# Attention scores of two query tiles at once, from the two halves of TensorE's rows

## The chip, the cores and the metric

The kernel runs on one core of a Trainium2 chip. The metric is the device time of one execution in microseconds (us). The core has five engines with instruction streams of their own: TensorE (PE in the profile, its weight loads PEld), VectorE (DVE), ScalarE (ACT), GpSimd (POOL) and SyncE (SP), which issues nearly all DMAs. TensorE multiplies 128 rows at a time: the stationary operand (the weights) is loaded, the moving operand streams past, and the result lands in PSUM, of which a bank holds 512 float32 per partition.

## The reference

One layer of a bidirectional encoder on a grid of 16 x 64 tokens (1024 tokens, width 1024), in float32. An embedding LayerNorm is followed by one combined input projection; its columns are the query, key, value and gate of a neighbourhood attention, the input and gate of a bidirectional gated recurrence, and two merge gates. What the change touches is the attention:

```
q_rows = (q * scale).reshape(B, rows, GRID_W, H, Dh).transpose(1, 0, 2, 3, 4)
...
s = jnp.einsum('bqhd,bqnhd->bhqn', q_row, k_g).astype(jnp.float32) + bias[None]
p = jax.nn.softmax(s, axis=-1).astype(v.dtype)
return jnp.einsum('bhqn,bqnhd->bqhd', p, v_g)
```

There are 8 heads of 64 channels. Each token attends to a window of 8 x 16 tokens of the grid. Afterwards both branches are gated, projected, merged and projected again, and a last LayerNorm ends the layer.

## The kernel before, in words

**Precision.** Matrix products use the type float32r, which carries fewer bits than float32. Operands are therefore split in a high part and a low part (`lo_of`, line 119, makes the low part), and a product is made of three: high x high, low x high, high x low (`mm3`, line 122).

**Stages.** Up to about 110 us the kernel normalises x, turns it with TensorE and projects v and q. `q_hi`, `q_lo` and `q_store` (lines 327 to 338) write each 128-row block of q, its high and low parts side by side, to a DRAM tensor `q_d`, for one half of the tokens (512) at a time. From there to 430 us the 16 pairs of the remaining column blocks are projected by a table of seven products per pair, one per slot of about 2.7 us; among them `take_k` (line 651) splits k and writes it to `k_d` (line 666). The recurrence's work is threaded between these slots. From 430 to 541 us comes the attention, then the branch projections and the output projection with the last LayerNorm.

**Tiles of the attention.** The 1024 tokens are eight tiles of 128 (a strip of 8 grid columns). A query tile's keys lie in its own strip and its neighbours (`near`, line 51): three key tiles, or two at the ends. For head h, `load_q` puts the high part of q (64 rows) and the low part (64 rows) on top of each other, so that a tile `qs` has all 128 rows in use; `load_k` reads k twice, so that `ks` has the high part of k in both row halves, and behind it the low part in both. `score` (line 1026) then needs two products of 128 rows: stacked q against high k, and stacked q against low k. The sum has all four of high x high, low x high, high x low and low x low.

**Order of the attention.** One loop (line 1145) runs over units, eight per head, with one head of lead-in and three units (`PV_LAG`) at the end. TensorE executes in the order written; the other engines as well. In the unit (h, c) stand, in this order:

- VectorE reads the score of the unit before out of PSUM, adds the bias and takes the row minimum of the negative (`biased`, line 1033); it belongs to head h + 1
- VectorE makes the low part of the transposed probabilities of the unit before (`turned_lo`)
- TensorE transposes probabilities of head h (`turned`) and multiplies those of three units ago with v (`values`, line 1067)
- ScalarE makes the high part (`turned_hi`), then the exponential (`exped`, line 1044)
- TensorE makes one `score` of head h + 1; which query tile is in the table `SCORES`
- at the first unit of a head, SyncE issues the loads for head h + 2
- TensorE makes "fill" products, which belong to the other branch's projection (tile `mb`): 2 or 2.5 per unit, by the table `FILL`

In the lead-in (head 0's scores) only scores and fill products stand on TensorE. Scores have two PSUM buffers (tag "s"), and a product into one waits until VectorE has read it. The score tiles `sc` in SBUF have two buffers too. Once per head `sums_turned` (line 1094) turns the row sums with a product of 8 weight columns.

Of the kernel before, what the change touches and what calls it, by code (L numbers as in the profile page):

```python
# [9 lines left out]
F32 = mybir.dt.float32  # L10
F32R = mybir.dt.float32r
# [3 lines left out]
P = 128  # L15
S = 1024
D = 1024
NK = D // P
H = 8
DH = 64  # L20
GR, GC = 16, 64
NT = S // P
HALF = 512
# [13 lines left out]
HI_POOL = ("a12", "s2", "s1", "s3", "s4")  # L37
U_PAIRS = (0, 5)
BLOCKS = (1, 0, 6, 2, 3, 4, 5, 7)
SCORES = (0, 1, 2, 5, 6, 7, 3, 4)  # L40
PV_LAG = 3
FILL = (16, 20, 20, 20, 20, 20, 20, 20, 12)

# [3 lines left out]
HALVES = ((slice(0, 64), slice(64, P)), (slice(64, P), slice(0, 64)))  # L47
# [3 lines left out]
def near(t):  # L51

    return range(max(t - 1, 0), min(t + 2, NT))
# [13 lines left out]
def encoder_kernel(ctx, tc, x, gb1, gb, w_qk, w_v, w_s, w_ba, w_bb, w_gate, smalls, bias, w_out, out):  # L67
    nc = tc.nc
    V, A, G, PE, SP = nc.vector, nc.scalar, nc.gpsimd, nc.tensor, nc.sync
# [7 lines left out]
    dram = tc.alloc_tile_pool(name="dram", bufs=1, space=bass.MemoryType.DRAM)  # L77
# [6 lines left out]
    def bank(name):  # L84
        return banks[0].tile([P, HALF], F32, tag="bank", name=name)

    h_d = dram.tile([NT, P, D], F32, name="h_d")
    v_d = dram.tile([4, P, NT, 4 * DH], F32, name="v_d")
    q_d = dram.tile([H // 2, P, 2, S], F32, name="q_d")
    k_d = dram.tile([H // 2, P, 2, S], F32, name="k_d")  # L90
    rs_d = dram.tile([H, NT, P], F32, name="rs_d")
    za_d = dram.tile([4, P, S], F32, name="za_d")
    zb_d = dram.tile([4, P, S], F32, name="zb_d")
# [25 lines left out]
    def lo_of(eng, lo, full, hi):  # L119
        eng.tensor_tensor(lo, full, hi.bitcast(F32), ALU.subtract)  # L120
# [70 lines left out]
    halves = [slice(c * HALF, (c + 1) * HALF) for c in range(2)]  # L191
# [59 lines left out]
    def ti(i):  # L251
        return slice((i % 4) * P, (i % 4 + 1) * P)
# [82 lines left out]

    def q_store(m, n):
        qs = outs.pop(("q", m, n))
        SP.dma_start(q_d[m][:, :, halves[n]], qs[:].bitcast(F32))


    s_a, s_w = {}, {}
# [102 lines left out]
    pst = tc.alloc_tile_pool(name="pst0", bufs=4, space=bass.MemoryType.PSUM, reuse_waits="tile")  # L444
# [206 lines left out]
    def take_k(m0):  # L651

        def consume(mi, n, add, o, c=None):
            c = o if c is None else c
            if add is not None:
                V.tensor_tensor(c[:], add[:], o[:], ALU.add)
            tag, w = ("uc", S) if (mi, n) == (1, 1) else ("up", S + 3)
            t = lru.tile([P, w], F32R, tag=tag, bufs=2, name=f"k{m0}{mi}{n}")
            hi, lo = t[:, :HALF], t[:, HALF:S]

            def high():
                A.copy(hi, c[:])

            def store():
                lo_of(V, lo, c[:], hi)
                SP.dma_start(k_d[m0 + mi][:, :, halves[n]], t[:, :S].rearrange("p (z f) -> p z f", z=2).bitcast(F32))
            return [high, store]
        return consume

# [178 lines left out]

    def load_q(h):
        hd = late["hd" if h % 2 else "hd0"]  # L850
        q = hd.tile([P, S], F32R, tag="qs", name=f"qs{h}")
        bt = hd.tile([P, BIAS_W], F32, tag="bias", name=f"bias{h}")
        SP.dma_start(q[:].bitcast(F32), q_d[h // 2][HALVES[h % 2][0]].rearrange("p z s -> (p z) s"))
        SP.dma_start(bt[:], bias[h])
        heads[h] = q, bt

    def load_k(h):
        k = late["hd"].tile([P, 2, S], F32R, tag="ks", bufs=2, name=f"ks{h}")
        SP.dma_start(k[:].rearrange("p z s -> p (z s)").bitcast(F32),
                     k_d[h // 2][HALVES[h % 2][0]].rearrange("p z s -> p (z s)").unsqueeze(1).to_broadcast([DH, 2, 2 * S]))  # L860
        heads[h] = heads[h][0], k, heads[h][1]

    def load_head(h):
# [109 lines left out]
    for slot in range(7 * N_PAIR + 4):  # L973
        p, k = divmod(slot, 7)
# [30 lines left out]
    pst = tc.alloc_tile_pool(name="pst", bufs=1, space=bass.MemoryType.PSUM, reuse_waits="tile")  # L1005
# [13 lines left out]
    vvs, sums, scs, tps, pts, attns, rsb, gates = {}, {}, {}, {}, {}, {}, {}, {}  # L1019
# [3 lines left out]
            vvs[hp] = at0.tile([P, NT, 2, 2 * DH], F32R, tag="vv", bufs=2, name=f"vv{hp}")  # L1023
            SP.dma_start(vvs[hp][:].rearrange("p b e c -> p b (e c)").bitcast(F32), v_d[hp])

    def score(h, t):
        q, k, _ = heads[h]
        keys = slice(near(t).start * P, near(t).stop * P)
        o = scs[h, t] = pst.tile([P, HALF], F32, tag="s", bufs=2, name=f"s{h}_{t}")
        for z in range(2):  # L1030
            PE.matmul(o[:, :P * len(near(t))], q[:, t * P:(t + 1) * P], k[:, z, keys], start=z == 0, stop=z == 1)  # L1031

    def biased(h, t):

# [9 lines left out]
    def exped(h, t):  # L1044
        w = P * len(near(t))
        A.activation(probs[h % 2][t][:], scs.pop((h, t))[:, :w], AF.Exp, bias=sums[h][0][:, t:t + 1], scale=-1.0,  # L1046
                     accum_out=sums[h][1][:, t:t + 1])
# [97 lines left out]
    for unit in range(-NT, H * NT + PV_LAG):  # L1145
        h, c = divmod(unit, NT)
        before, b = divmod(unit - 1, NT)
        pv, pb = divmod(unit - PV_LAG, NT)

        if -1 <= before < H - 1:  # L1150
            biased(before + 1, SCORES[b])
        if 0 <= before < H:
# [16 lines left out]
        if -1 <= before < H - 1:  # L1169
            exped(before + 1, SCORES[b])  # L1170
        for f in pending:
# [2 lines left out]
        for f in todo.pop(unit, ()):  # L1174
            f()
        if -1 <= h < H - 1:
            score(h + 1, SCORES[c])
        if 0 <= h < H:
            if c == (4 if h == H - 1 else 5 if h % 2 else 7):
                sums_in(h)  # L1180
# [50 lines left out]
    for slot in range(2 * NK + 2):  # L1231
        j, n = divmod(slot, 2)
# [12 lines left out]
        if j < NK:  # L1245
# [3 lines left out]
            o = sums_m[slot] = pst.tile([P, HALF], F32, tag="mb", bufs=2, name=f"mb0{n}") if slot < 2 else bank(f"mb{j}{n}")  # L1249
# [57 lines left out]
    for i in range(NT):  # L1307
        last = i == NT - 1
        load_z(i + 3)
        z = zs.pop(i)  # L1310
# [3 lines left out]
        for cols in [halves[0]] + (pieces[2:] if last else [halves[1]]):  # L1314
            o = o_product(i, cols)
# [110 lines left out]
```

## Time and profile before

| | |
|---|---|
| runs | 686.56, 683.94, 686.44 us; median 686.44 |
| profiled execution | 684.15 us, span 682.4 us |
| granted TensorE clock | 0.996 |
| busy: TensorE, weight loads, VectorE, ScalarE, GpSimd | 666.3, 555.0, 495.0, 364.0, 353.8 us |
| score products (line 1031) | 128, of 339 ns (384 columns) and 285 ns (256 columns) |
| DMA | 113.39 MB, mean 166 GB/s |

A row of the timeline gives start, time, engine, line, operation, output and inputs, weights' shape and moving shape; "x2" stands for two instructions after one another. A product's recorded time reaches to its modelled end, and the next starts before it; the distance of the starts is what a product holds of TensorE. What stands in brackets is idle time of the engine just before, and what ended it.

### The profile page before, as it was taken

What the parts mean: (1) busy time and instruction counts of PE and PEld (TensorE: products, weight loads), DVE (VectorE), ACT (ScalarE), POOL (GpSimd) and SP (SyncE); (2) the same over time, 40 slices, a digit from 0 to 9 for tenths busy, and PEclk for the clock granted to TensorE, in tenths of its full rate; (3) what the DMA queues carried; (4) which work ended last, traced back from release to release, by engine and by line L of the source; (5) the groups of instructions that cost most, each with busy time, mean ns of one, the idle gap of its engine ahead of it and who ended that gap; (6) DMA issues with size and microseconds to landing.
All of it is one profiled execution on the core that took longest, in us unless ns stands there. A gap on an engine that the chain in (4) does not pass through costs nothing.

```text
span 682.4 us, 9299 instructions
## 1 busy us (share of the span) xinstructions
PE 666.3 (98%) x3177; PEld 555.0 (81%) x3177; DVE 495.0 (73%) x821; ACT 364.0 (53%) x612; POOL 353.8 (52%) x258
## 2 busy tenths in 40 slices
PE   8999999999999999999999999999999999999995
PEld 6787888888888888888788888888888878888884
DVE  7866766796899599879977785377788777533434
ACT  4553524247686677768576635477777544310110
POOL 5697451344576577567647534115255446435442
PEclk9999999999999999999999999999999999999998
DMA  8754164233424133531453457898794557512211
GB/s 314 241 187 154 63 233 169 78 92 124 124 93 147 68 109 110 183 124 47 170 198 114 174 175 262 293 371 304 257 322 141 179 192 279 183 62 93 92 62 61
DMA packets 48702, 113.39 MB, mean 166 GB/s; under 512 B 5056, under 2 KB 9744, under 8 KB 47120
## 3 DMA queue, kind: packets, MB, share of 16 engines
q1 hardware_dynamic: 48624, 112.81, 47.6%
q8 instruction: 25, 0.41, 0.2%
q14 instruction: 21, 0.17, 0.1%
q10 hardware_dynamic: 32, 0.01, 0.0%
HBM read 77.11 MB, written 35.68 MB: 165 GB/s over the span
## 4 chain that ended last, share of the span: by engine, by line
PE 81%; DVE 8%; DMA 4%; POOL 3%; ACT 1%; issue 1%; SPq 1%; DVEq 0%; POOLq 0%; ACTq 0%
PE a L126 29%; PE o L126 13%; PE s L126 11%; PE mb L126 10%; PE q L126 5%; PE acc L1077 3%; PE s L1031 3%; PE pt L1053 2%; POOL x L238 2%; PE v L303 2%; PE g L729 2%; DMA wvsl<-in_w_v_dram 1%; DMA ks<-k_d 1%; DVE ws_l L120 1%; DVE uc L687 1%
## 5 line engine op out<-in xcount | busy, mean ns | idle before, releaser
L126 PE MATMUL o<-wo_h,ml 128*128 128x512 f32 (+1 forms) x136 | 51.2, 377 | 0.0
L126 PE MATMUL o<-wo_l,mh 128*128 128x512 f32 (+1 forms) x136 | 51.2, 376 | 0.0
L126 PE MATMUL o<-wo_h,mh 128*128 128x512 f32 (+1 forms) x136 | 51.2, 376 | 0.0
L126 PE MATMUL a<-ht_h,ws_h 128*128 128x512 f32 x128 | 50.0, 390 | 0.0
L126 PE MATMUL a<-ht_h,ws_l 128*128 128x512 f32 x128 | 49.8, 389 | 0.0
L126 PE MATMUL a<-ht_l,ws_h 128*128 128x512 f32 x128 | 49.8, 389 | 0.0
L126 PE MATMUL a<-b_h,wa_h 128*128 128x512 f32 x128 | 49.8, 389 | 0.0
L126 PE MATMUL a<-b_h,wa_l 128*128 128x512 f32 x128 | 49.8, 389 | 0.0
L126 PE MATMUL a<-b_l,wa_h 128*128 128x512 f32 x128 | 49.8, 389 | 0.0
L1041 DVE CUSTOM_DVE_ANT_0 sc<-s,bias 128x384 f32<-128x384 f32 (+1 forms) x64 | 33.4, 522 | 22.4 <-PE s L1031 14.0
L1316 DVE SCALAR_TENSOR_TENSOR z<-z,o 128x512 f32<-128x512 f32 (+1 forms) x17 | 11.2, 656 | 51.1 <-PE o L126 51.1
L1061 ACT CAST pt_h<-pt 128x384 fp32r<-128x384 f32 x64 | 29.0, 454 | 25.8 <-PE pt L1053 17.9
L1326 POOL TENSOR_TENSOR z<-z,gb 128x1024 f32<-128x1024 f32 x7 | 16.8, 2396 | 48.7 <-ACT z L1325 48.7
L1046 ACT ACTIVATE p<-sc,summ 128x384 f32<-128x384 f32 (+1 forms) x64 | 37.8, 591 | 5.2 <-DVE summ L1041 5.0
L1295 ACT ACTIVATE sd<-mv,eps_z 128x1 f32<-128x1 f32 x8 | 2.4, 294 | 67.1 <-DVE mv L1321 67.1
L303 PE MATMUL v<-wv,b_h 128*128 128x512 f32 x128 | 32.8, 398 | 2.7 <-ACT b_h L258 1.6
L120 DVE TENSOR_TENSOR pt_l<-pt,pt_h 128x384 fp32r<-128x384 f32 x64 | 33.2, 519 | 2.1 <-ACT pt_h L1061 1.6
L1031 PE MATMUL s<-ks,qs 128*128 128x384 f32 (+1 forms) x128 | 31.3, 326 | 0.5 <-DMA ks<-k_d 0.5
L837 POOL CAST wb_h<-wb 128x512 fp32r<-128x512 f32 x9 | 7.0, 780 | 47.5 <-DMA wb<-in_w_bb_dram 29.6
L303 PEld LDWEIGHTS v<-wv,b_h 128*128 128x128 f32 x128 | 23.6, 188 | 9.2 <-ACT b_h L258 2.3
L120 POOL TENSOR_TENSOR wb_l<-wb,wb_h 128x512 fp32r<-128x512 f32 x16 | 22.2, 1388 | 16.4 <-ACT wb_h L835 15.6
L1053 PEld LDWEIGHTS pt<-ident,p 128*128 128x128 f32 x176 | 23.1, 140 | 8.6
(438 smaller groups left out, 2201.3 us busy)
## 6 DMA issues: line engine op xcount, KB each, us to landing
ks<-k_d SPq DMA_DIRECT2D x8, 1024.0 KB, 8.0
h_d<-x SPq DMA_DIRECT2D x8, 512.0 KB, 4.5
v_d<-vs SPq DMA_DIRECT2D x8, 512.0 KB, 4.0
q_d<-q SPq DMA_DIRECT2D x8, 512.0 KB, 3.0
ga_d<-ga SPq DMA_DIRECT2D x16, 256.0 KB, 2.0
gb_d<-gb SPq DMA_DIRECT2D x16, 256.0 KB, 2.1
k_d<-k SPq DMA_DIRECT2D x8, 512.0 KB, 4.0
qs<-q_d SPq DMA_DIRECT2D x8, 512.0 KB, 5.5
```

The costliest lines, as they stand in the source:

```text
L120: eng.tensor_tensor(lo, full, hi.bitcast(F32), ALU.subtract)
L126: PE.matmul(o, a, b, start=first and i == 0, stop=last and i == len(prods) - 1, skip_group_check=not (first and last))
L238: G.tensor_tensor(z[:, halves[c]], z[:, halves[c]], gb_t[w][c][:], op)
L303: PE.matmul(vos[i][:], a, wv[kind == "w"][k][:], start=vn[i] == 0, stop=vn[i] == 23)
L729: PE.matmul(o[:, n, :], w[:, 2 * d + b, :], us[b][:, n * HALF:(n + 1) * HALF], start=z == 0, stop=z == 1)
L1031: PE.matmul(o[:, :P * len(near(t))], q[:, t * P:(t + 1) * P], k[:, z, keys], start=z == 0, stop=z == 1)
L1041: V.tensor_tensor_reduce(s[:, :w], o[:, :w], heads[h][2][:, b0:b0 + w], -1.0, 3.0e38, ALU.add, ALU.min, accum_out=sums[h][0][:, t:t + 1])
L1046: A.activation(probs[h % 2][t][:], scs.pop((h, t))[:, :w], AF.Exp, bias=sums[h][0][:, t:t + 1], scale=-1.0, accum_out=sums[h][1][:, t:t + 1])
L1053: PE.transpose(tp[:, n * P:(n + 1) * P], probs[h % 2][t][:, z * P:(z + 1) * P], ident[:])
L1061: A.copy(pt[0][:, span(b)], tps[h, b][:, :P * len(near(b))])
L1077: PE.matmul(acc[g][:, d:d + w], vvs[h // 2][:, b, h % 2, :], pt[:, a:a + w], start=b in (1, 6) and z == 0, stop=z == 1 and b == (4, 7)[g])
L1326: G.tensor_tensor(z[:], z[:], gb2[:, 0, :], ALU.mult)
```

## The change

`score(h, t)` becomes `scores(h, *ts)`, called in every second unit with two query tiles, t and t + 4 (the table `SCORES` pairs them). It makes three products for each: high x high, low x high, high x low, of 64 rows each; low x low is left out. The query tiles 0 to 3 have q and k in rows 0 to 63, the tiles 4 to 7 in rows 64 to 127, and the products of the two tiles alternate. For that, `q_d` holds for each head the first half of the tokens (64 rows, high and low part) and the second half apart, and `load_q` puts them above one another; `k_d` holds each head's k twice, so that each k store writes twice as much, from one tile of SBUF, and `load_k` fills all 128 rows from it in two DMAs, one for the high part and one for the low.

```diff
-SCORES = (0, 1, 2, 5, 6, 7, 3, 4)
+SCORES = (0, 4, 1, 5, 2, 6, 3, 7)
...
-    q_d = dram.tile([H // 2, P, 2, S], F32, name="q_d")
-    k_d = dram.tile([H // 2, P, 2, S], F32, name="k_d")
+    q_d = dram.tile([H, 2, DH, 2, HALF], F32, name="q_d")
+    k_d = dram.tile([H, 2, DH, 2, 2, HALF], F32, name="k_d")
...
-        SP.dma_start(q_d[m][:, :, halves[n]], qs[:].bitcast(F32))
+        for e in range(2):
+            SP.dma_start(q_d[2 * m + e][n], qs[HALVES[e][0]].bitcast(F32))
...
-                SP.dma_start(k_d[m0 + mi][:, :, halves[n]], t[:, :S].rearrange("p (z f) -> p z f", z=2).bitcast(F32))
+                for e in range(2):
+                    SP.dma_start(k_d[2 * (m0 + mi) + e][:, :, n].rearrange("y p z f -> p y (z f)"),
+                                 t[HALVES[e][0], :S].bitcast(F32).unsqueeze(1).to_broadcast([DH, 2, S]))
...
-        q = hd.tile([P, S], F32R, tag="qs", name=f"qs{h}")
+        q = hd.tile([P, 2, HALF], F32R, tag="qs", name=f"qs{h}")
...
-        SP.dma_start(q[:].bitcast(F32), q_d[h // 2][HALVES[h % 2][0]].rearrange("p z s -> (p z) s"))
+        SP.dma_start(q[:].rearrange("p z s -> p (z s)").bitcast(F32),
+                     q_d[h].rearrange("y p z s -> (y p) (z s)"))
...
-        SP.dma_start(k[:].rearrange("p z s -> p (z s)").bitcast(F32),
-                     k_d[h // 2][HALVES[h % 2][0]].rearrange("p z s -> p (z s)").unsqueeze(1).to_broadcast([DH, 2, 2 * S]))
+        for z in range(2):
+            SP.dma_start(k[:, z, :].rearrange("p (n f) -> p n f", n=2).bitcast(F32),
+                         k_d[h].rearrange("y p n z f -> (y p) n z f")[:, :, z, :])
...
-    def score(h, t):
+    def scores(h, *ts):
+
         q, k, _ = heads[h]
-        keys = slice(near(t).start * P, near(t).stop * P)
-        o = scs[h, t] = pst.tile([P, HALF], F32, tag="s", bufs=2, name=f"s{h}_{t}")
-        for z in range(2):
-            PE.matmul(o[:, :P * len(near(t))], q[:, t * P:(t + 1) * P], k[:, z, keys], start=z == 0, stop=z == 1)
+        for t in ts:
+            scs[h, t] = pst.tile([P, HALF], F32, tag="s", bufs=2, name=f"s{h}_{t}")
+        for z, (a, b) in enumerate(((0, 0), (1, 0), (0, 1))):
+            for t in ts:
+                rows, keys = HALVES[t // 4][0], slice(near(t).start * P, near(t).stop * P)
+                PE.matmul(scs[h, t][:, :P * len(near(t))], q[rows, a, ti(t)], k[rows, b, keys], start=z == 0, stop=z == 2)
...
-            score(h + 1, SCORES[c])
+            if c % 2 == 0:
+                scores(h + 1, *SCORES[c:c + 2])
```

Three places show how this moves instructions. The first is TensorE in the lead-in, before and then with the change (`s_2` is the score tile of query tile 2, `mb` a fill product):

```order
L1031 MATMUL s_1_4078<-ks_3933,qs_3871 128x384 x2
L126 MATMUL mb_4070<-yb_l,wb_h 128x512
L126 MATMUL mb_4070<-yb_h,wb_h 128x512
L1031 MATMUL s_2_4086<-ks_3933,qs_3871 128x384 x2
L126 MATMUL mb_4070<-yb_h,wb_l 128x512
```

```order
L126 MATMUL mb_4093<-yb_h,wb_h 128x512
L126 MATMUL mb_4093<-yb_h,wb_l 128x512
L126 MATMUL mb_4093<-yb_l,wb_h 128x512
L126 MATMUL mb_4093<-yb_h,wb_h 128x512
L1039 MATMUL s_1_4106<-ks_3949,qs_3887 128x384
L1039 MATMUL s_5_4107<-ks_3949,qs_3887 128x384
L1039 MATMUL s_1_4106<-ks_3949,qs_3887 128x384
L1039 MATMUL s_5_4107<-ks_3949,qs_3887 128x384
L1039 MATMUL s_1_4106<-ks_3949,qs_3887 128x384
L1039 MATMUL s_5_4107<-ks_3949,qs_3887 128x384
```

Two products of one tile after every two fill products have become six products, of two tiles in turn, after every four.

The second is TensorE in the steady stage, behind the unit that turns the row sums (`pt` is a tile of transposed probabilities, `acc` a sum of values), before and then with the change:

```order
L1077 MATMUL acc_4037<-pt_l,vv_4063 128x384
L1031 MATMUL s_5_4209<-ks_4020,qs_4016 128x384 x2
L126 MATMUL mb_4123<-yb_l,wb_h 128x512
L126 MATMUL mb_4219<-yb_h,wb_h 128x512
L126 MATMUL mb_4219<-yb_h,wb_l 128x512
L1053 MATMUL pt_3_4225<-ident,p_2_4041 128x128
L1053 MATMUL pt_3_4225<-ident,p_3_4042 128x128
L1053 MATMUL pt_3_4225<-ident,p_4_4043 128x128
L1077 MATMUL acc_4037<-pt_0_h,vv_4063 128x256
L1077 MATMUL acc_4037<-pt_0_l,vv_4063 128x256
L1031 MATMUL s_6_4235<-ks_4020,qs_4016 128x384 x2
```

```order
L1085 MATMUL acc_4055<-pt_l,vv_4081 128x384
L126 MATMUL mb_4152<-yb_l,wb_h 128x512
L126 MATMUL mb_4250<-yb_h,wb_h 128x512
L126 MATMUL mb_4250<-yb_h,wb_l 128x512
L1061 MATMUL pt_3_4256<-ident,p_2_4059 128x128
L1061 MATMUL pt_3_4256<-ident,p_3_4060 128x128
L1061 MATMUL pt_3_4256<-ident,p_4_4061 128x128
L1085 MATMUL acc_4055<-pt_0_h,vv_4081 128x256
L1085 MATMUL acc_4055<-pt_0_l,vv_4081 128x256
L1039 MATMUL s_2_4266<-ks_4037,qs_4033 128x384
L1039 MATMUL s_6_4267<-ks_4037,qs_4033 128x384
```

The unit that had a score of its own has none now, and the next has those of two tiles (the last row is followed by the other four products of the pair).

The third is SyncE where it loads head 1 (`qs`, `bias` and `ks`) and the values `vv`, before and then with the change:

```order
L853 DMA qs_4016<-q_d 128x1024
L854 DMA bias_4017<-in_bias_dram 128x896
L859 DMA ks_4020<-k_d 128x1x2048
L1024 DMA vv_4063<-v_d 128x2048
L937 DMA g_4068<-gb_d 128x512
L937 DMA g_4121<-gb_d 128x512
```

```order
L856 DMA qs_4033<-q_d 128x1024
L858 DMA bias_4034<-in_bias_dram 128x896
L864 DMA ks_4037<-k_d 128x2x512 x2
L1029 DMA vv_4081<-v_d 128x2048
L942 DMA g_4091<-gb_d 128x512
L942 DMA g_4150<-gb_d 128x512
```

One load of k has become two, each of half the columns in pieces of 512, in the same place of the queue.

## The prediction

> **What bounds the kernel now.** The page's first part is read first, then the stretches of the attention stage (from the first score product at 435.6 us to the last value product at 541.05), then the instructions in it. A row of a stretch gives its length, the busy time of TensorE, its weight loads, VectorE, ScalarE and GpSimd (counts in brackets), the granted clock, the DMA engines' busy share and GB/s.
>
> ```profile
> PE 666.3 (98%) x3177; PEld 555.0 (81%) x3177; DVE 495.0 (73%) x821; ACT 364.0 (53%) x612; POOL 353.8 (52%) x258
> ...
> 435.60:442.00 6.40, 6.40 (x34) 5.60 (x33) 4.76 (x16) 4.35 (x13) 1.91 (x2) 1.00 0.97 366
> 442.00:455.00 13.00, 12.51 (x79) 10.94 (x78) 9.06 (x29) 8.83 (x28) 0.00 (x0) 1.00 1.01 395
> 455.00:525.00 70.00, 69.98 (x435) 61.75 (x433) 54.26 (x158) 52.92 (x150) 31.65 (x31) 1.00 0.76 268
> ```
>
> TensorE has work in 69.98 of 70.00 us between 455 and 525, with VectorE and ScalarE under 78%, at a granted clock of 1.00. A busy TensorE may hide waits inside its pipeline, so the starts are what counts. Two pieces of its timeline, one of the lead-in (scores of head 0 and fill products alone), one of the steady stage:
>
> ```profile
> 437.13 0.52 PE L1031 MATMUL s<-ks,qs 128*128 128x384 f32 x2
> 437.48 0.40 PE L126 MATMUL mb<-yb_h,wb_l 128*128 128x512 f32 x1
> 437.72 0.40 PE L126 MATMUL mb<-yb_l,wb_h 128*128 128x512 f32 x1
> ...
> 449.38 0.49 PE L1053 MATMUL pt<-ident,p 128*128 128x128 f32 x3
> 449.62 0.48 PE L1077 MATMUL acc<-pt_h,vv 128*128 128x512 f32 x1
> 449.94 0.34 PE L1077 MATMUL acc<-pt_l,vv 128*128 128x384 f32 x1
> 450.12 0.40 PE L1031 MATMUL s<-ks,qs 128*128 128x256 f32 x2
> 450.36 0.40 PE L126 MATMUL mb<-yb_h,wb_l 128*128 128x512 f32 x1
> ```
>
> Each group starts where the one before leaves off. So this stage is paid in TensorE starts, and a cheaper score saves its full price until something else is late. A score of three key tiles costs 437.48 - 437.13 = 0.35 us (two products, 0.175 each), one of two key tiles 450.36 - 450.12 = 0.24. Of the 64 scores 48 are of the first kind and 16 (the first and last tile of each head) of the second: 48 x 0.35 + 16 x 0.24 = 16.8 + 3.8 = **20.6 us**, the whole sum that the change can work on.
>
> **The change, part by part.**
>
> *Scores in pairs.* 128 products of 128 rows become 192 of 64 rows, as 32 pairs of three steps; in a step the two tiles take different row halves and different PSUM banks. The trace has no 64-row product, so the price of a pair has bounds. Below: both halves run at once and a step takes what its wider product takes, 0.175; every pair has a 384-column member, so 3 x 0.175 = 0.525, and 32 pairs make 16.8 us, **-3.8 us**. Above: the halves run one after the other, 3 x 0.24 / 2 + 3 x 0.175 = 0.885 for the 16 pairs with a 256-column member and 1.05 for the other 16, 31.0 us, +10.4. I take the lower end: different rows, different banks and no operand in common leave nothing that the trace shows to be shared but the loading of weights, which is a rival below.
>
> [...]
>
> *The array's shape.* Each pair sits between 128-row work, so the shape of the array changes twice per pair. The nearest row is the product that turns the row sums (8 weight columns where all others have 128), once per head:
>
> ```profile
> 446.09 0.49 PE L1053 MATMUL pt<-ident,p 128*128 128x128 f32 x3
> 446.42 0.27 PE L1096 MATMUL pt<-ident,sums 128*8 128x128 f32 x1
> 446.45 0.48 PE L1077 MATMUL acc<-pt_h,vv 128*128 128x512 f32 x1
> 446.77 0.34 PE L1077 MATMUL acc<-pt_l,vv 128*128 128x384 f32 x1
> 446.94 0.52 PE L1031 MATMUL s<-ks,qs 128*128 128x384 f32 x2
> ```
>
> From the transposes to the score it is 0.85 us here and 450.12 - 449.38 = 0.74 in the same unit without it: 0.11 us, of which its own slot as a transposing product is 0.24 / 3 = 0.08. The two changes of shape cost 0.03, or at most 0.11 where its own slot is taken as free: 1.0 us over 32 pairs, at most 3.5. The other bound is that the array runs empty at each change. A steady product holds 2.72 / 12 = 0.227 us and is recorded with 0.389:
>
> ```profile
> 117.95 2.72 PE s L126 x12
> ...
> L126 PE MATMUL s<-ht_h,ws_h 128*128 128x512 f32 x64 | 24.9, 389 | 0.0
> ```
>
> That leaves 0.16 us of tail that a successor now overlaps; twice per pair it is 0.32, or 10.2 us. With the first weights of each shape loaded only after that (0.11, below) it is 0.54, or 17.3. I take 0.03, **+1.0 us**, since the one change of shape in the trace shows no such tail; but it narrows columns and not rows, so the others stay in the range.
>
> *Score buffers.* There are two PSUM buffers for scores, as before, but a pair fills both, so the next pair must wait until VectorE has read both. In the lead-in:
>
> ```profile
> 436.86 0.56 DVE L1041 CUSTOM_DVE_ANT_0 sc<-s,bias 128x384 f32<-128x384 f32 x1
> 437.35 0.08 DVE L1041 DVE_READ_ACCUMULATOR2_ANT summ<- 128x1 f32 x1
> 437.79 0.56 DVE L1041 CUSTOM_DVE_ANT_0 sc<-s,bias 128x384 f32<-128x384 f32 x1 [0.36 <-PE s L1031]
> 438.28 0.08 DVE L1041 DVE_READ_ACCUMULATOR2_ANT summ<- 128x1 f32 x1
> ```
>
> VectorE begins 437.79 - 437.48 = 0.31 us after TensorE has moved on from the score, and a read takes 0.57 (436.86 to the end of its 437.35 row). Two reads end 0.31 + 1.14 = 1.45 after the pair; TensorE has four fill products, 4 x 0.23 = 0.92, before the next pair. It waits 0.5 us three times in the lead-in, and about 0.2 twice where head 0's first transposes start: **+1.9 us**. Queued behind the waiting score are the fill products, then the transposes and value products. In the steady stage two units (about 3.2 us) lie between pairs: after 0.525 for the pair 2.7 us are left, against 0.31 + 1.14 for the reads and about one 0.5 us low-half subtraction and one 0.6 us gate or merge between them, 2.6. That holds on average; a heavy unit would add 0.1 here and there.
>
> *Order of scores.* Tile 7 is now scored last, in unit 6, and its first transpose is in unit 2 of the next head, over three units later; what must lie between is one 0.57 us read and one exponential of about 0.8 us. No cost. VectorE waits for scores 28 times before, so later scores find slack there:
>
> ```profile
> DVE sc L1041 <- PE s L1031: 14.0, 28, 0.8
> ```
>
> *DMA.* Each q store becomes two of half the rows, each k store two with every row written twice (4 MB more in all), each k load two.
>
> ```profile
> ks<-k_d SPq DMA_DIRECT2D x8, 1024.0 KB, 8.0
> k_d<-k SPq DMA_DIRECT2D x8, 512.0 KB, 4.0
> L859 SPq DMA_DIRECT2D ks<-k_d x8: 525/528/552, 422.2 to 506.1; - x8
> ...
> 77.00:110.00 33.00, 33.00 (x147) 27.35 (x146) 21.40 (x25) 12.52 (x22) 15.60 (x10) 1.00 0.51 176
> 327.00:381.00 54.00, 53.63 (x237) 44.05 (x236) 44.42 (x50) 36.63 (x47) 32.67 (x22) 1.00 0.48 166
> ```
>
> The stores fall where the DMA engines are half idle (0.51 and 0.48), and their readers come 40 us later: the k stores' 4 MB more in 54 us lift 166 GB/s to some 245, still below the 395 reached at 442 to 455. Cover gone, a store's 4 us would show, but only if its reader waited. SyncE pays about 0.5 us for each added issue, past stores and loads that are wanted two slots later. What is tight is head 1's k:
>
> ```profile
> 434.67 8.11 DMA ks<-k_d
> 442.92 0.47 PE L1031 MATMUL s<-ks,qs 128*128 128x256 f32 x2 [0.49 <-DMA ks<-k_d]
> ```
>
> Its second half is issued 0.5 us later on full DMA engines, so it lands at 443.2 or later. TensorE, delayed by 1.5 us of buffer waits and quicker by 4 x (0.70 - 0.525), arrives 0.8 us later than the 442.43 of before. The wait of 0.49 shrinks to 0 to 0.4: **-0.3 us**.
>
> **Sum.** -3.8 + 1.0 + 1.9 - 0.3 = -1.2 us, on the profiled execution's own 684.15 (span 682.4): 682.9. That execution lies 2.3 us below the median of the runs, 686.44, so the prediction is 686.4 - 1.2 = **685.2**: no change that can be told, half a per cent (3.4 us) being about what a measurement of this kernel separates. Its own terms give 682.5 (no shape cost, waits of 1.0) to 688 (0.11 per pair).
>
> **The rivals.**
>
> *The array empties at every change* (slower). The price is 0.32 us per pair in place of 0.03, up to 0.54: -3.8 + 10.2 + 1.9 - 0.3 = +8.0, 694.4, and 701.5 at the upper end. It decides from about 0.2 us per pair on. The sum-turning product speaks against it, its different kind of shape for it. Chance 0.18. [...]
>
> *Weights set the pace* (slightly slower). A pair now loads weights six times where two scores loaded four.
>
> ```profile
> 483.23 0.19 PEld L1077 LDWEIGHTS acc<-pt_h,vv 128*128 128x128 f32 x1
> 483.34 0.19 PEld L1077 LDWEIGHTS acc<-pt_l,vv 128*128 128x128 f32 x1
> 483.46 0.30 PEld L1031 LDWEIGHTS s<-ks,qs 128*128 128x128 f32 x2
> ```
>
> Loads follow each other at 0.115 us; if the two halves share the loader and gain nothing from half the rows, a pair takes 0.69: 22.1 us, +1.5 + 1.0 + 1.9 - 0.3 = +4.1, 690.5. For it: nothing before had loads this dense. Chance 0.14. [...]
>
> *The halves run in turn*, so the change doesn't do what it says: +10.4 + 1.0 + 1.9 - 0.3 = +13.0, 699.4. Chance 0.08.
>
> *A clear gain.* If half-height products lose their margin over 2.72 / 12 us per 512 columns (0.17 for 384, 0.51 per pair, -4.3), shape changes are free, and half the buffer waits vanish under VectorE's idle time: -4.3 + 1.0 - 0.5 = -3.8, 682.6. Chance 0.15.
>
> **How the numbers follow.** The forecast has 0.45. Below 683.0 (faster by over 0.5%) lie 0.13 of the clear gain and 0.11 of the forecast: 0.24. Above 689.9 lie 0.18 + 0.08 + 0.08 of the weights: 0.34. Between: 0.42. The range of 8 in 10 is 681 to 696; it leaves out the turn-taking case, the upper end of the emptying array, and gains beyond 5 us.
>
> **What would show it.** Score products of a pair recorded with starts a few ns apart, and about 0.55 us from the first of a pair to the next fill product, prove the first two terms; 0.7 means weights, 0.85 and more with gaps at both edges means emptying, 1.0 with alternating starts means turns. Waits of score products for VectorE's reads, some 0.5 us, three times before 443 us, prove the buffer term; if they recur through 455 to 525, the steady slack was misjudged. The work before 435 us should take as long as before; were it longer, the stores had cover that I misread, and the prediction fails elsewhere.

## The result, and the profile after

The changed kernel takes 697.67 us (median of 4 runs, 695.57 to 699.74), the kernel before 686.47 in the same comparison: a ratio of 1.0176, 95% interval 1.0156 to 1.0196. By the medians it is slower by 11.2 us, where a time of 685.2 was forecast. The profiled execution of after has 698.64 us (span 696.9), 14.5 more than that of before.

Where the 14.5 us arose is read from the same products in both traces:

| first product of | before | after | later by |
|---|---|---|---|
| projection of q (no changed instruction yet) | 40.34 | 41.37 | 1.0 |
| the 16 projected pairs | 109.63 | 110.75 | 1.1 |
| attention (first score) | 435.61 | 441.34 | 5.7 |
| the branch projection behind the attention | 541.05 | 554.06 | 13.0 |
| the output projection | 586.9 | 601.4 | 14.5 |

So 1.1 us belong to the start, which differs from execution to execution; 4.6 to the projections, where the stores of k lie; 7.3 to the attention; and 1.5 come behind it, which the last section tells.

**The attention.** The page's first part and the windows of after answer to the first rows of the prediction. TensorE is still busy without a gap, at a clock of 1.00, and its weight loads are busy for less time (54.74 of 70 us, where it was 61.75).

```profile
PE 676.7 (97%) x3241; PEld 549.8 (79%) x3241; DVE 496.5 (71%) x821; ACT 364.2 (52%) x612; POOL 354.9 (51%) x258
...
441.34:455.00 13.66, 13.66 (x77) 9.43 (x77) 8.71 (x31) 8.37 (x26) 1.90 (x2) 1.00 1.00 367
455.00:525.00 70.00, 70.00 (x447) 54.74 (x445) 50.16 (x145) 48.47 (x138) 25.29 (x24) 1.00 0.87 289
```

The timeline of TensorE after, a piece of the lead-in and one of the steady stage (start, duration, engine, line, operation; x6 is a whole pair):

```profile
441.34 0.79 PE L1039 MATMUL s<-ks,qs 64*128 64x256 f32 x6
442.05 0.50 PE L126 MATMUL mb<-yb_h,wb_h 128*128 128x512 f32 x1
442.39 0.39 PE L126 MATMUL mb<-yb_h,wb_l 128*128 128x512 f32 x1
442.62 0.39 PE L126 MATMUL mb<-yb_l,wb_h 128*128 128x512 f32 x1
...
472.68 0.34 PE L1085 MATMUL acc<-pt_l,vv 128*128 128x384 f32 x1
472.94 0.79 PE L1039 MATMUL s<-ks,qs 64*128 64x384 f32 x6
473.66 0.50 PE L126 MATMUL mb<-yb_h,wb_h 128*128 128x512 f32 x1
474.00 0.40 PE L126 MATMUL mb<-yb_h,wb_l 128*128 128x512 f32 x1
```

From the first score product of a pair to the next fill product it is 473.66 - 472.94 = 0.72 us; three steps at 0.175 would be 0.525. And the products at both edges hold TensorE longer than elsewhere: the value product ahead 0.26 (472.68 to 472.94) where 384 columns take 0.17, the fill product behind 0.34 (473.66 to 474.00) where the next takes 0.23 (442.39 to 442.62). On the average of the 32 pairs, two waits for buffers aside, a pair holds TensorE for 0.09 + 0.72 + 0.10 = 0.91 us: what the product ahead loses, the pair itself, and what the fill product behind loses. Of that, 0.39 is neither of its streams. The two scores that it replaces held 0.66. The loads of weights in the same place:

```profile
472.50 0.19 PEld L1085 LDWEIGHTS acc<-pt_l,vv 128*128 128x128 f32 x1
472.94 0.47 PEld L1039 LDWEIGHTS s<-ks,qs 64*128 64x128 f32 x6 [0.25 <-issue]
473.66 0.19 PEld L126 LDWEIGHTS mb<-yb_h,wb_h 128*128 128x128 f32 x1 [0.25 <-issue]
473.77 0.19 PEld L126 LDWEIGHTS mb<-yb_h,wb_l 128*128 128x128 f32 x1
```

Among products of one shape the weights are loaded ahead: those of the value product of 472.68 at 472.50, those of the fill product of 474.00 at 473.77. At both changes of shape the loading stands idle, here for 0.25 us, and begins when its product is recorded to begin (472.94, 473.66), so nothing is loaded ahead there. Over the 32 pairs it is 0.25 us behind each pair and 0.13 to 0.36 ahead of it, by the kind of the product before.

**The projections.** The DMA engines' share and GB/s are the last two numbers of a window's row. First before, then after:

```profile
340.00:350.00 10.00, 10.00 (x46) 8.29 (x45) 7.87 (x12) 8.70 (x10) 6.28 (x6) 1.00 0.84 280
350.00:360.00 10.00, 10.00 (x46) 8.29 (x45) 6.48 (x10) 6.44 (x9) 2.86 (x4) 1.00 0.24 89
```

```profile
340.00:350.00 10.00, 9.11 (x41) 7.26 (x40) 9.64 (x14) 5.26 (x7) 4.16 (x5) 1.00 0.86 250
350.00:360.00 10.00, 10.00 (x46) 8.25 (x45) 4.00 (x4) 7.57 (x11) 4.42 (x4) 1.00 0.92 248
360.00:370.00 10.00, 9.49 (x43) 7.53 (x42) 7.72 (x8) 6.73 (x9) 5.10 (x4) 1.00 0.27 101
```

After, the DMA engines are nearly full at 248 GB/s, and TensorE has gaps. SyncE's own timeline shows what comes late, the weights `a_12f` and then `a_13f` of later projections, before and then after:

```profile
328.46 2.45 SPq L346 DMA_DIRECT2D a_12f<-in_w_s_dram  x4
...
343.09 0.53 SPq L666 DMA_DIRECT2D k_d<-k  x1
343.71 0.56 SPq L647 DMA_DIRECT2D ga_d<-ga  x1
344.36 2.49 SPq L346 DMA_DIRECT2D a_13f<-in_w_s_dram  x4
```

```profile
330.74 4.99 SPq L347 DMA_DIRECT2D a_12f<-in_w_s_dram  x4
...
347.64 4.15 SPq L668 DMA_DIRECT2D k_d<-k  x2
351.89 1.55 SPq L648 DMA_DIRECT2D ga_d<-ga  x1
353.55 3.29 SPq L347 DMA_DIRECT2D a_13f<-in_w_s_dram  x4
```

The two DMAs of one k store keep SyncE for 4.15 us, and `a_13f` is issued 9.2 us later. The chain of waits of after goes through it. VectorE waits 8 us for it, and 2.1 us for `a_12f`, which stands behind an earlier k store and takes 4.99 us to issue instead of 2.45 (the chain, then the waits view: total, times, longest):

```profile
356.42 5.74 DMA a_13f<-in_w_s_dram
```

```profile
DVE s_13f L355 <- DMA a_13f<-in_w_s_dram: 8.0, 1, 8.0
DVE s_12f L355 <- DMA a_12f<-in_w_s_dram: 2.1, 1, 2.1
```

The chain of before runs through this stretch in TensorE's products alone. Set against the same products of before, TensorE of after falls back by 1.1 us at 349 us, ahead of `a_13f`, and by 2.4 us at 367 and 375, behind it; the rest of the 4.6 comes in smaller steps. So `a_13f` is the larger part, not the whole.

### The profile page after: what moved, and what is told of

Its sections match the earlier page's. It is cut to its first block, busy times and chain, and to the rows that moved or that the text cites. A ratio compares the mean times of both kernels' runs of the same rounds, so it can differ in the third digit from the quotient of the medians.

```text
span 696.9 us, 9428 instructions
## 1 busy us (share of the span) xinstructions
PE 676.7 (97%) x3241; PEld 549.8 (79%) x3241; DVE 496.5 (71%) x821; ACT 364.2 (52%) x612; POOL 354.9 (51%) x258
## 4 chain that ended last, share of the span: by engine, by line
PE 71%; DVE 12%; DMA 5%; POOL 3%; issue 3%; ACT 2%; SPq 2%; DVEq 0%; POOLq 0%; ACTq 0%
PE a L126 21%; PE mb L126 13%; PE o L126 13%; PE s L126 8%; PE q L126 5%; PE s L1039 3%; PE acc L1085 3%; PE pt L1061 3%; POOL x L238 2%; DVE ws_l L120 2%; PE v L303 2%; DMA wvsl<-in_w_v_dram 2%; SPq L347 1%; PE g L732 1%; DVE wa_l L120 1%
## 5 line engine op out<-in xcount | busy, mean ns | idle before, releaser
L1325 DVE SCALAR_TENSOR_TENSOR z<-z,o 128x512 f32<-128x512 f32 (+1 forms) x17 | 11.2, 656 | 51.0 <-PE o L126 51.0
L1061 PE MATMUL pt<-ident,p 128*128 128x128 f32 x176 | 29.6, 272 | 0.0
```

The source lines that it names most:

```text
L1061: PE.transpose(tp[:, n * P:(n + 1) * P], probs[h % 2][t][:, z * P:(z + 1) * P], ident[:])
L1325: V.scalar_tensor_tensor(z[:, cols], z[:, cols], ALPHA * TWICE, o, ALU.mult, ALU.add)
```

## The experiments: the two halves of the change apart

**Stores alone.** The scores of before, the stores of after; the loads adapted (k read in four pieces).

```diff
...
-                SP.dma_start(k_d[m0 + mi][:, :, halves[n]], t[:, :S]...)
+                for e in range(2):
+                    SP.dma_start(k_d[2 * (m0 + mi) + e][:, :, n]..., t[HALVES[e][0], :S]...to_broadcast([DH, 2, S]))
```

> The scores of the kernel before (two products of 128 rows per tile), with the changed kernel's q and k stores: from 64 rows each, k written twice; the loads are adapted to that layout (k in four pieces). Theory of the stores (they keep the DMA engines full from 330 to 360 us, so the projection's weights come late): the first score begins 4 to 5 us later than the 435.6 us of before, the attention itself takes the 105.4 us it took before, and the kernel is 4 to 6 us slower than before, 690.5 to 692.5. Rival (the late start in the changed kernel was chance, or came from elsewhere): 686 to 687.5, first score at 435 to 437 us.

Measured: 688.88 us, ratio 1.0059 (1.0034 to 1.0084). That is 3.8 us above before in the same comparison (685.08), a little under the expected 4 to 6. The first score is 4.7 us later than before. The projected pairs of this execution began 0.3 us later already, so the delay is 4.4 net of the start, and later delays are given in this way too. The attention takes 105.8 us, as before (105.4). So the delay ahead of the attention comes from the stores, and about a third of the loss.

**Scores alone.** The paired scores of after, the stores of before; then q and k can only be loaded in DMAs of 64 rows.

```diff
...
+        for y in range(2):
+            SP.dma_start(k[HALVES[y][0]].bitcast(F32), k_d[h // 2][HALVES[h % 2][0]])
```

> The changed kernel's paired scores, with the stores of the kernel before (128 rows, k once); q and k are loaded in two DMAs each, one per row half. Theory of the array's shape (about 0.4 us at the two edges of each of 32 pairs): first score at 435.5 to 437 us, from the first score to the last value product 112 to 113.5 us against 105.4, and 7 to 9 us slower than before, 693.5 to 695.5. Rival (the stores cost it all, and the attention only looks longer because its loads come late): 686 to 688.

Measured: 711.5 us, ratio 1.0384 (1.0323 to 1.0445), a miss. The first score comes when it did before (435.90), so the delay of the projections has gone with the stores, which was expected. But the attention takes 132.1 us, as the k loads of 64 rows now come late. The chain of waits shows two of them; before, this load took 8.11 us.

```profile
437.07 11.79 DMA ks<-k_d
...
466.24 13.19 DMA ks<-k_d
```

Where no load is late, a pair takes 0.72 and the fill product behind it 0.335, as in after. What the pairs cost cannot be read from this time.

## The experiments: what a pair costs

**Both tiles of a pair in the same rows**, so that the products can't run at once and all else is equal.

```diff
-SCORES = (0, 4, 1, 5, 2, 6, 3, 7)
+SCORES = (0, 1, 2, 3, 4, 5, 6, 7)
```

> The changed kernel with the pairs (0,1), (2,3), (4,5), (6,7): both tiles of a pair lie in the same 64 rows. If the two halves' products run together in the changed kernel, they now run in turn: 16 pairs longer by 0.36 us and 16 by 0.525, about 14 us slower than the changed kernel's 697.7, some 712. If they ran in turn before, no change: 697 to 699.

Measured: 708.89 us, ratio 1.0341 (1.0308 to 1.0374).

```profile
471.98 1.31 PE L1039 MATMUL s<-ks,qs 64*128 64x384 f32 x6
473.23 0.50 PE L126 MATMUL mb<-yb_h,wb_l 128*128 128x512 f32 x1
```

A pair now takes 1.25 us, or 1.08 where one tile has 256 columns: 0.53 and 0.36 more than the 0.72 of after, which is 3 x 0.175 and 3 x 0.12. So in the change the products of different halves do run at once. The edges stay as in after: a value product of 384 columns ahead holds 0.27, the fill product behind 0.33. The time is 3 us under the expected 712. In the traces the attention does grow by nearly the expected 14, from 112.7 to 126.4 us. But the projected pairs begin 1.7 us earlier here than in the profiled execution of after, and the 1.5 us that after lost behind the attention (last section) are not lost here.

**All 128 rows in the six products.** Each product multiplies both halves of the rows, so that it sums the scores of two tiles, which is not what the reference computes; order, buffers and the number of products and loads stay.

```diff
-                PE.matmul(scs[h, t][:, ...], q[rows, a, ti(t)], k[rows, b, keys], ...)
+                PE.matmul(scs[h, t][:, ...], q[:, a, ti(t)], k[:, b, keys], ...)
```

> The changed kernel with all 128 rows in each of its six products per pair (a score is then the sum of two tiles' products with their own halves, so this computes something else in the same order, waits and bytes). No change of the array's shape is left, and the products run in turn. Theory of the array's shape: the edges' 0.4 us per pair go (-12.5), the streams cost 14 us more, so 698 to 701, and the fill products behind a pair start 0.23 us apart, not 0.34. Rival (the edges come from waiting for PSUM buffers or from six products in a row): the edges stay and it takes about 712.

Measured: 699.62 us, ratio 1.0206 (1.0173 to 1.0238).

```profile
472.13 0.34 PE L1085 MATMUL acc<-pt_l,vv 128*128 128x384 f32 x1
472.30 1.05 PE L1039 MATMUL s<-ks,qs 128*128 128x384 f32 x6
473.20 0.40 PE L126 MATMUL mb<-yb_h,wb_h 128*128 128x512 f32 x1
473.44 0.39 PE L126 MATMUL mb<-yb_h,wb_l 128*128 128x512 f32 x1
```

The edges have gone: 0.17 ahead, 0.24 behind, and the pair takes 0.89 or 1.05, just the sum of its six streams. The time is within the expected range. Six products in turn without edges cost nearly as much as six at once with them. That puts the 0.39 us on the change of the shape, and not on the number of loads, the order or the buffers.

**Four changes of shape per pair in place of two.** One fill product is moved inside the pair, behind its first step.

```diff
         for z, (a, b) in enumerate(((0, 0), (1, 0), (0, 1))):
+            if z == 1 and next(fill, True) is None:
+                filled += 1
...
```

> The changed kernel with one fill product moved between the first and the second step of each pair, so the array's shape changes four times per pair and not twice; the work is the same. Theory of the shape: 0.40 us more for each pair, 12 to 13 us, less where a wait for PSUM buffers is covered: 708 to 711. Rival (the edges belong to the pair's begin and end, as waits, not to the shape): 697 to 699.

Measured: 711.98 us, ratio 1.0388 (1.0357 to 1.0419): 14.3 us above the 697.67 of after, 0.45 per pair and just above the expected range.

```profile
476.93 0.43 PE L1042 MATMUL s<-ks,qs 64*128 64x384 f32 x2
477.30 0.49 PE L126 MATMUL mb<-yb_h,wb_h 128*128 128x512 f32 x1
477.72 0.62 PE L1042 MATMUL s<-ks,qs 64*128 64x384 f32 x4
478.27 0.50 PE L126 MATMUL mb<-yb_h,wb_l 128*128 128x512 f32 x1
```

One step and its edge take 0.37 where the step has 0.175 of work, and the fill product between two pieces holds 0.42 where it needs 0.23. In the steady stage that is 0.39 per pair again, so two more changes cost as much as the first two: the price goes by the change.

Together these three runs give a price of 0.2 us per change between 128-row and 64-row products; the weights that are then not loaded ahead are part of it. What else TensorE does in that time, no trace shows.

## The experiments: what made the stores late

The k store differs from before in four ways: 64 rows instead of 128, double the bytes, more issues on SyncE, and pieces of 4 KB. Five runs take these apart. In four of them the scores are those of before.

**64 rows, same bytes.** Each k store of before as two DMAs.

```diff
+                for e in range(2):
+                    SP.dma_start(k_d[m0 + mi][HALVES[e][0], :, halves[n]], t[HALVES[e][0], :S]...)
```

> The kernel before with each k store cut in two DMAs of 64 rows; same bytes, same layout, as many issues as the changed kernel makes. Theory of the rows (a store from 64 rows moves at half the rate, so these take as much DMA time as twice the bytes would): its packets of 2 KB take about 160 ns, not 85; the k stores hold the DMA engines about 10 us longer in all, and the first score comes 0 to 1.5 us late: 685 to 687. Theory of the issues (SyncE's added issues and their waits delay the loads behind them, whatever the bytes): 4 us late as in the kernel with the changed stores, 689 to 690.

Measured: 685.48 us, ratio 1.0003 (0.9991 to 1.0015). The time is the expected one, the packets are not. From 320 to 420 us, where all k stores lie, the median packet of 2 KB takes 84 ns; 1142 of 6911 take over 130, where before has 384 of 6904. Together these packets fill the 16 engines for 4.5 us more, not 10. The half rate of 64 rows, on which that theory rests, is not what this run shows.

**Double the bytes, 128 rows.** Each k store of before a second time, to a tensor `k_e` that nobody reads.

```diff
+                for d in (k_d, k_e):
+                    SP.dma_start(d[m0 + mi][:, :, halves[n]], t[:, :S]...)
```

> The kernel before with each k store made a second time, whole (128 rows), to a tensor that nobody reads: the bytes and the issues of the changed kernel's k stores at full width. Theory of the rows: packets stay at 85 ns, the added DMA time is about 10 us, and the first score comes 0 to 1.5 us late: 685 to 687. Theory that the doubled bytes or issues do it alone: 4 us late, 689 to 690.

Measured: 685.03 us, ratio 0.9995 (0.998 to 1.001). So neither alone costs anything, and neither does a second DMA per store.

**Both together**, in pieces of 2 KB: the loops over `d` and `e` nested, four issues in place of one.

> The kernel before, with each k store made twice (to k_d and to a second tensor that nobody reads), and each of the two as two DMAs of 64 rows: half the rows and double the bytes together, in pieces of 2 KB. If it is this combination that delays the projections (each alone cost nothing), the first score comes 3 to 5 us late and the time is 688 to 690.5. If it is the 4 KB pieces, in which the change reads each row twice, or the place of the bytes, it is 685 to 687 and the first score comes when it did.

Measured: 687.87 us, ratio 1.0038 (1.0021 to 1.0055), first score 2.3 us late net of the start. Both are below what was expected for the combination, but the delay is clear.

**The same four issues, bytes and pieces with whole rows**: high and low part apart, in place of the two halves.

```diff
+                for d in (k_d, k_e):
+                    for z in range(2):
+                        SP.dma_start(d[m0 + mi][:, z, halves[n]], t[:, z * HALF:(z + 1) * HALF].bitcast(F32))
```

> The kernel before, with each k store made twice (to k_d and to a second tensor that nobody reads), and each of the two as two DMAs of all 128 rows, one for the high part and one for the low: the same four issues, the same doubled bytes and the same 2 KB pieces as in the run with half rows, but whole rows. If 64 rows are what takes the time, the first score comes within 1 us of before, TensorE is busy without a gap from 340 to 370, and the time is 685 to 686.5. If it is the four issues on SyncE (each next transfer waits behind them), the first score is 2 to 3 us late and the time 687 to 689, as it was with half rows.

Measured: 685.03 us, ratio 0.9998 (0.9984 to 1.0012). The same window and the issue of `a_13f` on SyncE, first with half rows and then with whole rows:

```profile
340.00:350.00 10.00, 9.27 (x41) 7.40 (x40) 9.97 (x13) 6.30 (x7) 4.59 (x4) 1.00 0.80 238
350.00:360.00 10.00, 10.00 (x45) 8.27 (x45) 2.91 (x5) 6.97 (x10) 3.61 (x5) 1.00 0.90 292
...
351.81 2.55 SPq L347 DMA_DIRECT2D a_13f<-in_w_s_dram  x4
```

```profile
340.00:350.00 10.00, 10.00 (x46) 8.28 (x45) 7.85 (x12) 8.58 (x10) 6.25 (x6) 1.00 1.01 331
350.00:360.00 10.00, 10.00 (x45) 8.29 (x45) 6.57 (x10) 6.43 (x9) 2.92 (x4) 1.00 0.39 144
...
346.22 2.27 SPq L347 DMA_DIRECT2D a_13f<-in_w_s_dram  x4
```

With whole rows `a_13f` is issued 5.6 us earlier, and TensorE has no gap. But the two runs differ in more than the rows. With whole rows the DMA of the high part leaves before the low part is made (the first at 322.88 us, where the first with half rows leaves at 328.11), so fewer issues stand right ahead of `a_12f`, which is issued at 329.36 in place of 331.18. And 331 against 238 GB/s is for the most part idle time of the DMA engines, whose busy share is 1.01 against 0.80: a packet of 2 KB takes 96 ns on average with whole rows and 103 with half rows (320 to 420 us).

What the runs show is this. Half rows and double bytes together come late, with two DMAs per store (stores alone) as with four, and two DMAs with one of them alone do not. In the late ones (after, stores alone, both together, and one whole store and two halves below) VectorE waits 1.3 to 2.1 us for `a_12f` and 5.8 to 8.0 for `a_13f`; in the runs of this section that are not late, at most 0.2 and 1.7. That the lower rate of the halves is the reason, more than the moment at which SyncE gets to the next weights, is not shown: the packets' 103 against 96 ns point that way, but other transfers are mixed in.

The 2.3 us are half of the 4.4 of the change. Its 4 KB pieces take 258 ns each (the median of the trace's 1024 between 327 and 366 us). Those between 75 and 112 us, most of them of q's stores and from 64 rows too, take 159. So 64 rows and 4 KB alone do not make a piece this slow; whether it is the rows read twice or the transfers beside them, no run takes apart.

**The changed kernel with the k stores issued by ScalarE**, so that SyncE is not held by them.

```diff
-                    SP.dma_start(k_d[2 * (m0 + mi) + e][:, :, n]...
+                    A.dma_start(k_d[2 * (m0 + mi) + e][:, :, n]...
```

> The changed kernel with its k stores issued by ScalarE, so SyncE's queue has only the loads of the projection's weights and the gate stores. If the weights are late because they stand behind the stores in SyncE's queue: first score at 436 to 438 us, not 440 to 441, and 693 to 695.5 in all. If the DMA engines are simply full, whoever asks: first score at 440 us or later, 697 to 699; ScalarE's issues cost it 0.5 us each, at worst 2 us more.

Measured: 706.03 us, ratio 1.0297 (1.0275 to 1.0319): 8 us worse than the change, a miss of both theories. A store stands in ScalarE's order behind VectorE's low part of k, and ScalarE waits there with all that comes after it, among it a copy for which TensorE waits. The bracket of the first row names the next instruction of VectorE; the low part ended at 339.55 us, the store was issued at 339.58, and the copy followed:

```profile
340.87 0.58 ACT L913 COPY u<-a 128x512 f32<-128x512 f32 x1 [6.68 <-DVE s_12f L355]
```

```profile
337.08 0.39 PE L126 MATMUL a<-b_l,wa_h 128*128 128x512 f32 x1
341.60 0.77 PE L126 MATMUL a<-ht_h,ws_h 128*128 128x512 f32 x1 [4.12 <-ACT u L913]
```

The first score comes 14 us late net of the start. The run says nothing on the rate of half rows.

## The experiments: the change without its store delay

**Whole rows, k_d turned.** Two k stores of 128 rows each, every row still written twice; a head's k is then read as two blocks of 64 rows of DRAM in one DMA.

```diff
-    k_d = dram.tile([H, 2, DH, 2, 2, HALF], F32, name="k_d")
+    k_d = dram.tile([H // 2, 2, P, 2, S], F32, name="k_d")
...
+                for z in range(2):
+                    SP.dma_start(k_d[m0 + mi][:, :, z, halves[n]]..., t[:, z * HALF:(z + 1) * HALF]...to_broadcast([P, 2, HALF]))
...
```

> The change, with the layout of k_d turned so that a k store still writes each row twice but as two DMAs of all 128 rows (one for the high part, one for the low, pieces of 2 KB), and a head's k is read in one DMA. The paired scores stay. If half rows are what made the stores late, the projection stage takes as long as before, the first score comes within 1 us of before, and the time is the changed kernel's less some 4: 692.5 to 695, all of the rest being the pairs. If the doubled bytes did it, 697 to 699 and a first score 4 to 5 us late.

Measured: 829.62 us, ratio 1.2111 (1.2078 to 1.2145), far outside both ranges. The stores do what was expected: TensorE has no gap from 340 to 400 us, of which this is the first third. But a load of k, 1 MB as before, now takes up to 27.78 us in place of 8.11, and every head waits for it; the first score comes at 446.30 us, not within 1 us of before:

```profile
340.00:360.00 20.00, 20.00 (x90) 16.56 (x89) 14.46 (x21) 14.56 (x18) 9.59 (x8) 1.00 0.70 237
```

```profile
451.68 27.78 DMA ks<-k_d
```

```profile
PE s L1038 <- DMA ks<-k_d: 116.5, 8, 20.7
```

This load has two blocks of 64 rows outermost. The next run, whose load has 128 rows outermost, has no wait for k, but it changes the layout in other ways too; so what makes the load slow is not shown.

**One whole store and two halves.** k_d has 256 rows per pair of heads (second copy of one head, both heads, second copy of the other), so that a store is one DMA of 128 rows and two of 64 in 2 KB pieces, and a load 128 rows that follow each other.

```diff
-    k_d = dram.tile([H, 2, DH, 2, 2, HALF], F32, name="k_d")
+    k_d = dram.tile([H // 2, 2 * P, 2, S], F32, name="k_d")
...
+                for out, rows in ((slice(DH, 3 * DH), slice(0, P)), (slice(0, DH), HALVES[0][0]), (slice(3 * DH, 4 * DH), HALVES[1][0])):
+                    SP.dma_start(k_d[m0 + mi][out, :, halves[n]], t[rows, :S]...)
...
```

> The change, with k_d laid out as 256 rows per pair of heads (second copy of one head, both heads, second copy of the other), so that a k store is one DMA of all 128 rows and two of 64 rows, in pieces of 2 KB, and a head's k is read in one DMA of 128 consecutive rows. The paired scores and the doubled bytes stay. If 64-row stores of 4 KB pieces make the projections late, most of it goes: TensorE without gaps from 340 to 370, a first score 0 to 2 us late, and the time is the changed kernel's less 2.5 to 4.5: 693 to 695.5, the rest of the loss being the pairs. If the doubling as such delays them behind k loads and weights, 696 to 699 and a first score 4 to 5 us late.

Measured: 693.53 us, ratio 1.0117 (1.01 to 1.0135): 4 us better than the change and inside the expected range. But the delay has not gone as expected: TensorE is busy for 9.27 of the 10 us from 340 to 350, and the first score is 2.2 us late net of the start, half of the change's delay. The attention takes 112.7 us as in after, with pairs of 0.72. The best form of the change that was found still loses to before, by its pairs.

## Why the prediction was wrong, and where it was right

**Products at once: right.** Streams of 0.525 per pair were taken, -3.8 us; the records of a pair's first two products start 3 ns apart, and the pairs in the same rows showed what turn-taking would have cost (+11.2 over the change).

**"The two changes of shape cost 0.03": wrong, and the main failed step.** They cost 0.39 per pair, 12.5 us in place of 1.0. The row it was taken from, the product that turns the row sums, narrows the columns of the weights and keeps all 128 rows; its 0.11 us said nothing on a change of rows. The rival of the emptying array put a price on each change, as the runs do, and its bounds of 0.32 to 0.54 hold it; it was given 0.18. That the array runs empty was its assumption: the traces show the weights loaded late, and nothing of the array itself. The text of the prediction had noticed that its row was of a "different kind of shape", and still took the row's number as the likeliest.

**"It waits 0.5 us three times ... about 0.2 twice": oversized.** The lead-in waits for score buffers 0.54 us in all (pairs of 0.92 and 1.06 in place of 0.72), where 1.9 was taken. In both, the second product begins 0.05 us after VectorE's read of that buffer has ended. The edges made TensorE itself slower by 0.39 per pair, and VectorE used that time. The two terms were not independent.

**"The stores fall where the DMA engines are half idle": wrong, the second failed step.** It cost 4.4 us in the trace, 3.8 in the runs of the stores alone. A mean of 0.48 over 54 us hid that 340 to 350 was already at 0.84; the rate of 395 GB/s that was taken as room came from other transfers, and the windows of after with these stores reached 250. Its "their readers come 40 us later" looked at the readers of k, where it was the next transfers in SyncE's order, the weights `a_12f` and `a_13f`, that came late. What these stores cost is shown; how it divides among rows, bytes and the order on SyncE stays open.

**The wait for head 1's k: right in direction.** It has gone (0.5 before, no such row after): TensorE reached head 1's first score 7.9 us behind head 0's, in place of the 6.8 of before, where it then waited.

**The test by 0.72 would have misled.** The prediction read "0.7 means weights, 0.85 and more with gaps at both edges means emptying". The pair took 0.72, yet its six loads took 0.47 us (row of 472.94), not 0.69; and with six full-height loads it lost no time beyond its streams. What the product ahead and the first fill product behind lose lies outside the stretch that was to be measured.

**Sum.** In the trace: streams -4.2, shape +12.5, buffers +0.5, and about 1.5 less elsewhere, 1.3 of it behind transposes, among it the wait for head 1's k. That makes the attention's +7.3; the stores +4.4. Together 11.7, beside 11.2 in the runs. With 12.5 in place of 1.0 the prediction's own sum would have come to 697, which looks right but would be luck: its waits were some 2.6 us too large and its saving of streams 0.4 too small, which covers 3.0 of the 4.4 of the stores that it left out. Two slips of the working changed nothing: the lower end of its own terms is 683.3 (-3.8 + 1.0 - 0.3), not 682.5, and two scores of head 0 hold 0.645 us on average, not 0.70, as two of its four pairs have a tile of 256 columns.

## What to carry to other kernels

In these runs two 64-row products side by side saved stream time (a pair of 0.72 us in place of 1.25 in turn) and cost 0.2 us at each edge with 128-row work; count the edges first, and pack only where many such products can stand together. A nearest row bounds a price only if it changes the same thing; where it changes another dimension, it speaks for no value, and the bounds should carry the chance. Judge room for a transfer in windows as short as the transfer, at the rate that its own form reaches, and look at what stands behind it in its queue, not only at its reader.

## What was not expected of the hardware

- Weights were not loaded ahead over a change between 128-row and 64-row products: the loading stood idle for 0.13 to 0.36 us ahead of a pair and 0.25 behind it, and TensorE lost 0.2 us per change.
- Stores of 64 rows cost nothing at single bytes (685.48 us beside 685.44), and doubled bytes cost nothing with 128 rows (685.03 beside 685.44); both together, in four DMAs per store, made the first score 2.3 us late.
- Behind the attention TensorE waits for ScalarE, before and after alike: it is idle for 1.66 us, and two products start 2.1 us apart. In the profiled execution of after its clock fell there (0.51 granted between 561 and 564 us, 0.97 between 555 and 605; before had 1.00 there and at its own wait, from 547 to 550):

```profile
558.75 0.50 PE L126 MATMUL mb<-ya_l,wb_h 128*128 128x512 f32 x1
560.91 0.67 PE L126 MATMUL mb<-ya_h,wb_h 128*128 128x512 f32 x1 [1.66 <-ACT ya_h L1130]
561.37 0.63 PE L126 MATMUL mb<-ya_h,wb_l 128*128 128x512 f32 x1
561.80 0.63 PE L126 MATMUL mb<-ya_l,wb_h 128*128 128x512 f32 x1
```

The products then start 0.43 apart, in place of 0.23, some eight times, which is the last 1.5 us of the 14.5. It happened in the seven traces where the two starts lie 2.16 us apart (after, k stores in two halves, scores alone, all 128 rows, four changes of shape, k_d turned, one whole store and two halves), and in none of the other seven (1.73 to 2.13 us; before, stores alone and same rows are among them). Since the k stores in halves, with the scores of before, have it and the pairs in the same rows have not, it isn't bound to paired scores. What makes the clock fall, no run settles.
